# Five store tiles of 26, 25, 26, 25 and 26 tokens in place of 25, 25, 25, 25 and 28 in an expert-dispatch scaling kernel

## The chip, the core and the metric

The kernel runs on one core of one Trainium2 chip. The metric is the device time of one execution in microseconds. Three runs of the kernel before took 238.78, 238.79 and 238.80 us; their median is 238.79 us.

## What is computed

Each token's row of 512 floats is written out twice, once for each of its two experts, and multiplied by that expert's weight. The expert indices are not used.

```python
def reference(x, expert_indices, expert_weights):   # x (16, 1024, 512), expert_weights (16, 1024, 2), float32
    k = expert_indices.shape[-1]
    x_expanded = x[:, :, np.newaxis, :].repeat(k, axis=2)
    weights = expert_weights[..., np.newaxis]
    return (x_expanded * weights).astype(np.float32)   # (16, 1024, 2, 512)
```

There are 16,384 tokens, 128 for each of the chip's 128 partitions. The input is 33.6 MB and the output 67.1 MB, so the work is nearly all transfer.

## The kernel before

The 128 tokens of each partition are cut into five tiles, `groups` (L32). In this text a "token" of a tile means one token on every partition: 256 KiB to load and 512 KiB to store. The tiles are numbered from 0, and a tile's two stored halves are called a and b: store 0a, store 0b, and so on.

**Buffers.** `x_pair` holds two input buffers; tiles 0, 2 and 4 use the first (x0), tiles 1 and 3 the second (x1). There is a single output buffer, `o_ring`, `TX` = 25 tokens long (L33, L47). Every tile writes its products into the same `o_ring`, and its first 13 tokens (`CUT`, L34) are stored as one transfer, the rest up to `TX` as a second. So the products of the first half of one tile must wait until store a of the tile before has landed, and those of the second half until its store b has landed.

**Products.** For each half, VectorE takes the first 8 tokens (9 in tile 0) in instructions of up to four tokens (`vector`, L113; the instruction itself is L97), and ScalarE the remaining ones, two instructions for each token (`scalar`, L118, L120).

**Loads.** A tile's load is cut into the steps of `STEPS` (L35): tile 0 in 9 and 16 tokens, tile 2 in 21 and 4, tile 4 in 24 and 4. The two pieces are called load 0a, load 0b and so on here. Tiles 1 and 3 are loaded whole.

**Order.** All transfers but the first weights go through one queue, SyncE's, in program order (`move`, L65, which issues at L66): load 0a, load 0b, load 1, load 2a, load 2b, the weights of tiles 1 to 4, store 0a, store 0b, store 1a, store 1b, load 3, load 4a, load 4b, store 2a, store 2b, store 3a, store 3b, store 4a, store 4b. An issue that has to wait holds back all that follow it. Tiles 0 and 2 are "held" (L140): their two stores are issued only after the next load into the same input buffer, and each also waits until piece a of that load has landed (`wait`, L69, called at L156). Piece b of that load, 4 tokens, is then still in the queue.

**The third piece.** Tile 4 has 28 tokens, three more than `o_ring` holds. For these, VectorE makes one product of three tokens into the start of `o_ring` (L161), which waits until store 4a has landed, and a third store (L162), called store 4c here, ends the program.

Of the kernel before, what the change touches and what calls it, by code (L numbers as in the profile page):

```python
# [1 line left out]

# [4 lines left out]


@with_exitstack
def kernel(  # L10
    ctx: ExitStack,
    tc: tile.TileContext,
    x: bass.AP,
    expert_indices: bass.AP,
    expert_weights: bass.AP,
    out: bass.AP,
):
    nc = tc.nc

    batch, seq, hidden = x.shape  # L20
    k = expert_weights.shape[-1]
    P = nc.NUM_PARTITIONS
    ntok = batch * seq
    assert ntok % P == 0
    A_TOTAL = ntok // P

    f32 = mybir.dt.float32
    row = k * hidden
    CH = 4


    groups = [25, 25, 25, 25, 28]  # L32
    TX = 25  # L33
    CUT = 13  # L34
    STEPS = {0: [9, 16], 2: [21, 4], 4: [24, 4]}  # L35
    assert sum(groups) == A_TOTAL

    xf = x.rearrange("b s h -> (b s) h")
    of = out.rearrange("b s k h -> (b s) (k h)")
    wf = expert_weights.rearrange("b s k -> (b s) k")  # L40

    w_pool = ctx.enter_context(tc.tile_pool(name="w_pool", bufs=1))
    x_pool = ctx.enter_context(tc.tile_pool(name="x_pool", bufs=1))
    o_pool = ctx.enter_context(tc.tile_pool(name="o_pool", bufs=1))

    w_tile = w_pool.tile([P, A_TOTAL * k], f32)
    o_ring = o_pool.tile([P, TX * row], f32)  # L47
    x_pair = [
        x_pool.tile([P, max(groups[e::2]) * hidden], f32, name=f"x{e}")
        for e in range(2)  # L50
    ]

    def rows(of_all, done, T):
        return of_all[done * P : (done + T) * P, :].rearrange(
            "(p a) n -> p (a n)", a=T
        )

    tiles = []
    done = 0
    for n in groups:  # L60
        tiles.append((done, n))
        done += n


    def move(out, in_):  # L65
        return tc.keep_in_program_order(nc.sync.dma_start(out=out, in_=in_))  # L66


    def wait(ins, done):  # L69
        tc.add_manual_dep(  # L70
            ins.ins,
            done.ins.name,
            mybir.DependencyInfo(
                mybir.DependencyClass.Sync, mybir.DependencyReason.DATA
            ),
            reason="turn",
        )

    def load(i, e):
        at = sum(STEPS.get(i, groups[i : i + 1])[:e])  # L80
        to = at + STEPS.get(i, groups[i : i + 1])[e]
        part = slice(at * hidden, to * hidden)
        return move(x_pair[i % 2][:, part], rows(xf, *tiles[i])[:, part])

    def weights(g, to):
        at, n = tiles[g]
        w = w_tile[:, at * k : (at + (to - g) * n) * k]
        return (
            w.rearrange("p (g m) -> p g m", g=to - g),
            wf[at * P : (at + (to - g) * n) * P, :].rearrange(  # L90
                "(g p a) n -> p g (a n)", g=to - g, p=P
            ),
        )

    def product(o_tile, t, x_in, c, m):
        o = t * row
        nc.vector.tensor_tensor(  # L97
            out=o_tile[:, o : o + m * row].rearrange(
                "p (t k h) -> p t k h", t=m, k=k
            ),  # L100
            in0=x_in[:, : m * hidden]
            .rearrange("p (t h) -> p t h", t=m)
            .unsqueeze(2)
            .to_broadcast([P, m, k, hidden]),
            in1=w_tile[:, c : c + m * k]
            .rearrange("p (t k) -> p t k", t=m)
            .unsqueeze(3)
            .to_broadcast([P, m, k, hidden]),
            op=mybir.AluOpType.mult,
        )  # L110


    def vector(src, c, at, to):  # L113
        for t in range(at, to, CH):
            u = min(t + CH, to)
            product(o_ring, t, src[:, t * hidden : u * hidden], c + t * k, u - t)

    def scalar(src, c, at, to):  # L118
        return [
            nc.scalar.mul(  # L120
                out=o_ring[:, e * hidden : (e + 1) * hidden],
                in_=src[:, e // k * hidden : (e // k + 1) * hidden],
                mul=w_tile[:, c + e : c + e + 1],
            )
            for e in range(at * k, to * k)
        ]

    def store(dst, at, to):
        return move(dst[:, at * row : to * row], o_ring[:, at * row : to * row])


    out_w, in_w = weights(0, 1)
    nc.scalar.dma_start(out=out_w, in_=in_w)
    load(0, 0)
    load(0, 1)
    load(1, 0)
    for i, (done, n) in enumerate(tiles):
        src, dst, c = x_pair[i % 2], rows(of, done, n), done * k
        v = 9 if i == 0 else 8
        held = i in (0, 2)  # L140
        for at, to in [(0, CUT), (CUT, TX)]:
            vector(src, c, at, at + v)
            scalar(src, c, at + v, to)
            if not held:
                store(dst, at, to)
        if held:
            if i == 0:
                last = load(2, 0)
                load(2, 1)
                for g in range(1, len(tiles)):  # L150
                    move(*weights(g, g + 1))
            else:
                last = load(4, 0)
                load(4, 1)
            for at, to in [(0, CUT), (CUT, TX)]:
                wait(store(dst, at, to), last)  # L156
        elif i == 1:
            load(3, 0)
        if n > TX:
            m = n - TX  # L160
            product(o_ring, 0, src[:, TX * hidden :], c + TX * k, m)  # L161
            move(dst[:, TX * row :], o_ring[:, : m * row])  # L162

# [1 line left out]
_INS = ['x', 'expert_indices', 'expert_weights']  # L165
_OUTS = [((16, 1024, 2, 512), 'float32')]


# [23 lines left out]
```

## Time and profile before

| | |
|---|---|
| median of three runs | 238.79 us |
| the profiled execution: whole time | 238.92 us |
| the profiled execution: span, first to last instruction | 237.1 us |
| VectorE busy | 93.1 us (39%), 23 instructions |
| ScalarE busy | 54.9 us (23%), 87 instructions |
| SyncE's transfer queue (q1) | 3312 packets, 100.77 MB, 98.7% of 16 engines' span |
| mean rate over the span | 425 GB/s |

The time outside the span, 238.92 less 237.1, is 1.8 us. "98.7%" is the time that the packets of this queue took, summed, as a share of what 16 DMA engines have in the span. The rows that carry the argument are shown in the prediction.

### The profile page before, as it was taken

Reading aid. Unit: us, or ns where it says so; the run is one execution under the profiler, and the core shown is the slowest. Engines: PE = TensorE matmul, PEld = TensorE weight load, DVE = VectorE, ACT = ScalarE, POOL = GpSimd, SP = SyncE. Lnnn points to the kernel's source line nnn. Section 1 sums busy time; section 2 is a strip of 40 time slices with the busy share of each in tenths; the row PEclk is TensorE's granted clock in tenths of the full one; section 3 lists DMA queues with packets and bytes.
Section 4 is the critical chain, followed back from the end, with each engine's and each line's share of the span. In section 5 each row is a group of like instructions: output and inputs, shape, how many; then the busy total and the mean of one; then the engine's idle time right before and its main releaser. Section 6 shows DMA issues by size and latency. Waiting matters only on the chain.

```text
span 237.1 us, 217 instructions
## 1 busy us (share of the span) xinstructions
DVE 93.1 (39%) x23; ACT 54.9 (23%) x87; POOL 0.2 (0%) x4
## 2 busy tenths in 40 slices
DVE  0499800000094580954900000039195292861300
ACT  0008800000090520914400000037080270800000
POOL 0000000000000000000000000000000000000000
DMA  7999989899999999999999999999999999999996
GB/s 260 474 445 475 423 370 464 372 486 431 420 398 497 464 431 420 398 398 409 475 478 406 398 453 431 431 409 457 484 431 431 409 398 434 449 449 456 423 398 265
DMA packets 3457, 100.80 MB, mean 425 GB/s; under 512 B 1024, under 2 KB 1024, under 8 KB 1024
## 3 DMA queue, kind: packets, MB, share of 16 engines
q1 hardware_dynamic: 3312, 100.77, 98.7%
q10 hardware_dynamic: 144, 0.03, 0.1%
q14 instruction: 1, 0.01, 0.0%
HBM read 33.69 MB, written 67.11 MB: 425 GB/s over the span
## 4 chain that ended last, share of the span: by engine, by line
DMA 70%; DVE 16%; ACT 4%; issue 3%; SPq 0%; DVEq 0%; ACTq 0%
DMA out_dram<-o_ring 46%; DMA x<-in_x_dram 24%; DVE o_ring L97 16%; ACT o_ring L120 3%; ACT L120 1%; SPq L66 0%; DVEq L97 0%; ACTq L120 0%
## 5 line engine op out<-in xcount | busy, mean ns | idle before, releaser
L97 DVE TENSOR_TENSOR o_ring<-x,w_tile 128x4096 f32<-128x4096 f32 (+2 forms) x23 | 93.1, 4096 | 128.5 <-DMA out_dram<-o_ring 105.6
L120 ACT ACTIVATE o_ring<-x,w_tile 128x512 f32<-128x512 f32 x86 | 53.7, 709 | 134.0 <-DMA out_dram<-o_ring 123.3
L120 ACT ACT_TABLE_LOAD x1 | 1.3, 1283 | 18.6 <-DMA x<-in_x_dram 18.6
L176 POOL MEMSET const-bfloat16-1.0<- 128x1 bf16 x1 | 0.1, 102 | 0.0
L176 POOL MEMSET const-uint8-127<- 128x1 uint8 x1 | 0.1, 102 | 0.0
L176 POOL MEMSET const-float32-0.0<- 128x1 f32 x1 | 0.1, 99 | 0.2 <-issue 0.2
L176 POOL MEMSET const-float32-1.0<- 128x1 f32 x1 | 0.1, 99 | 0.0
## 6 DMA issues: line engine op xcount, KB each, us to landing
out_dram<-o_ring SPq DMA_DIRECT2D x5, 6656.0 KB, 21.3
out_dram<-o_ring SPq DMA_DIRECT2D x5, 6144.0 KB, 21.6
x<-in_x_dram SPq DMA_DIRECT2D x2, 6400.0 KB, 34.1
x<-in_x_dram SPq DMA_DIRECT2D x1, 6144.0 KB, 20.6
x<-in_x_dram SPq DMA_DIRECT2D x1, 5376.0 KB, 18.8
x<-in_x_dram SPq DMA_DIRECT2D x1, 4096.0 KB, 17.4
x<-in_x_dram SPq DMA_DIRECT2D x1, 2304.0 KB, 8.1
x<-in_x_dram SPq DMA_DIRECT2D x2, 1024.0 KB, 21.4
```

The source lines that it names most:

```text
L97: nc.vector.tensor_tensor(out=o_tile[:, o : o + m * row].rearrange("p (t k h) -> p t k h", t=m, k=k), in0=x_in[:, : m * hidden] .rearrange ...
L120: nc.scalar.mul(out=o_ring[:, e * hidden : (e + 1) * hidden], in_=src[:, e // k * hidden : (e // k + 1) * hidden], mul=w_tile[:, c + e : c ...
L176: nc = _bacc.Bacc("TRN2", target_bir_lowering=False, num_devices=1)
```

## The change

The tiles become 26, 25, 26, 25 and 26 tokens, and `o_ring` 26 tokens. Each tile now fits in it, so each is stored in two pieces: 13 and 13 tokens, or 13 and 12. The branch with the third piece goes. Piece b of load 0 has 17 tokens instead of 16, load 2 comes in 22 and 4 tokens instead of 21 and 4, and load 4 in 22 and 4 instead of 24 and 4. The number of tokens that VectorE takes is left as it is, so the added tokens of tiles 0, 2 and 4 fall to ScalarE, two instructions each. Input buffer x0 shrinks from 28 to 26 tokens.

```diff
-    groups = [25, 25, 25, 25, 28]
-    TX = 25
+    groups = [26, 25, 26, 25, 26]
+    TX = max(groups)
     CUT = 13
-    STEPS = {0: [9, 16], 2: [21, 4], 4: [24, 4]}
+    STEPS = {0: [9, 17], 2: [22, 4], 4: [22, 4]}
...
-        for at, to in [(0, CUT), (CUT, TX)]:
+        for at, to in [(0, CUT), (CUT, n)]:
             vector(src, c, at, at + v)
             scalar(src, c, at + v, to)
...
-            for at, to in [(0, CUT), (CUT, TX)]:
+            for at, to in [(0, CUT), (CUT, n)]:
                 wait(store(dst, at, to), last)
         elif i == 1:
             load(3, 0)
-        if n > TX:
-            m = n - TX
-            product(o_ring, 0, src[:, TX * hidden :], c + TX * k, m)
-            move(dst[:, TX * row :], o_ring[:, : m * row])
```

## The prediction

> **What bounds the kernel now.** I read the page's parts on the span and the queues first, because a kernel that moves 100 MB should be judged by how full its transfer queue is.
>
> ```profile
> span 237.1 us, 217 instructions
> ...
> DMA  7999989899999999999999999999999999999996
> ...
> q1 hardware_dynamic: 3312, 100.77, 98.7%
> ```
>
> The second line is the busy share of the 16 DMA engines in 40 slices of the span: nine tenths or more nearly throughout. 98.7% of 237.1 us is 234.0 us, so the engines stood idle for 3.1 us in all. The view by stretches says where. Its columns are start and end, length, the three compute engines with their counts, the granted TensorE clock, the DMA share and GB/s; packets count where they begin.
>
> ```profile
> 0.00:1.00 1.00, 0.00 (x0) 0.00 (x0) 0.20 (x4) 1.00 0.00 0
> 235.00:237.10 2.10, 0.00 (x0) 0.00 (x0) 0.00 (x0) 1.00 0.14 59
> ```
>
> The first microsecond moves nothing. In the last 2.1 us the share is 0.14, so 0.86 x 2.1 = 1.81 us are idle. Of the 3.1 us, 1.0 + 1.81 = 2.81 lie at the two ends, and about 0.3 us are left for everything between. So a change that keeps the bytes can gain about 0.3 us from gaps, and can lose as much as it opens.
>
> Now the chain that ended last, in order of time (start, length, what). It would mislead if it were read alone.
>
> ```profile
> 27.64 18.75 DMA x<-in_x_dram
> ...
> 46.41 18.56 DMA out_dram<-o_ring
> ...
> 118.85 20.61 DMA x<-in_x_dram
> ...
> 139.52 18.14 DMA out_dram<-o_ring
> ...
> 188.08 8.77 DVE o_ring L97 x2
> ...
> 196.90 21.27 DMA out_dram<-o_ring
> ...
> 218.29 3.36 DVE o_ring L97
> ```
>
> Its last link is the very product that the change removes, 3.36 us of VectorE after store 4a landed at 196.90 + 21.27 = 218.17. The chain follows releases, and a transfer in it counts from its issue, queueing included. Whether the product cost anything is decided by what the queue still held, so I take landing times: issue plus time to landing. The issues of the last three stores, and what each took to land (the middle one asked for at 211 to 212 us):
>
> ```profile
> 211.39 10.62 SPq L66 DMA_DIRECT2D out_dram<-o_ring  x2
> ...
> out_dram<-o_ring SPq DMA_DIRECT2D x1, 6144.0 KB, 21.3
> ...
> 221.68 0.33 SPq L66 DMA_DIRECT2D out_dram<-o_ring  x1
> ...
> out_dram<-o_ring SPq DMA_DIRECT2D x1, 1536.0 KB, 14.7
> ```
>
> Store 4b landed at 211.39 + 21.3 = 232.69, store 4c at 221.68 + 14.7 = 236.38. Store 4c was thus issued 11.0 us before the queue was through with 4b. The product and the wait in front of it are covered.
>
> **The price of a byte.** From 218.17 to 232.69 the queue carried the 6144 KiB of store 4b and nothing else: 14.52 us, 433 GB/s. One token costs 0.605 us to load and 1.21 us to store. Thirteen stored tokens cost 15.73 us, four loaded ones 2.42.
>
> **What goes away.** The last store took 236.38 - 232.69 = 3.69 us for three tokens, which at the price above are 3.63. Its own packets, 3312 / 23 = 144 for one of the queue's 23 transfers, cost 0.06 us more. The same from the queue's view of the stretch 231.7 to 235.2, small packets, and then 142 to 156, large ones:
>
> ```profile
> DMA packets 135, 1.50 MB, mean 428 GB/s; under 512 B 13, under 2 KB 13, under 8 KB 13
> ...
> q1 hardware_dynamic: 135, 1.50, 100.4%
> ...
> DMA packets 112, 5.96 MB, mean 426 GB/s; under 512 B 0, under 2 KB 0, under 8 KB 0
> ...
> q1 hardware_dynamic: 112, 5.96, 98.3%
> ```
>
> 428 / 1.004 = 426.3 GB/s and 426 / 0.983 = 433.4 GB/s: 1.6% of 3.69 us is again 0.06. With the rounding of the landing times it is 0 to 0.12; I take **-0.06 us**. The product (3.36 us) and its issue go at no gain, because the cover is 11.0 us.
>
> The Trainium skill, SBUF — State Buffer, section "The DMA setup-cost knee", says that every transfer pays a roughly fixed 2 us, and advises the largest single transfers. By it one transfer less would give -2.0 us where it stands in line. The rows above leave 0.06: behind another transfer the fixed part is not seen.
>
> **What moves.** The bytes stay. Loads: tile 0 gains a token, tile 2 one (25 to 26 in all), tile 4 loses two. Stores: 0b, 2b and 4b grow by one token each, 3 x 1.21 = 3.63 us, the bytes of 4c. So the queue runs 0.61 us late after load 0b, 1.21 after load 2a, 2.42 after store 0b, 1.21 again after load 4a, 2.42 after store 2b, 3.63 after store 4b, where it ends and 4c used to follow: sum **0**, as long as no new gap opens. What each issue waits for, and what is in the queue meanwhile:
>
> ```profile
> 9.01 19.70 DVE L97 TENSOR_TENSOR o_ring<-x,w_tile 128x4096 f32<-128x4096 f32 x6 [9.01 <-DMA w_tile<-in_expert_weights_dram]
> ...
> 19.90 8.68 ACT L120 ACTIVATE o_ring<-x,w_tile 128x512 f32<-128x512 f32 x14
> ...
> 27.64 1.48 SPq L66 DMA_DIRECT2D x<-in_x_dram  x2
> 29.16 1.90 SPq L66 DMA_DIRECT2D w_tile<-in_expert_weights_dram  x4
> ...
> 1.16 0.90 SPq L66 DMA_DIRECT2D x<-in_x_dram  x2
> ...
> x<-in_x_dram SPq DMA_DIRECT2D x1, 6400.0 KB, 32.0
> ```
>
> *Tile 0.* Load 1 was issued by 2.06 and landed 32.0 us later, at 33.6 or after; it begins 0.61 later now. Load 2a, of 22 tokens, must also wait for VectorE's one-token product, whose end bounds the six: 9.01 + 19.70 = 28.71, at most 0.61 later, 29.3, against 27.64. That is 4.9 us before load 1 lands (34.2), more than the way from an issue to its bytes takes (2.65 us at most, below): hidden. ScalarE has 16 instructions for 14, 8.68 / 14 = 0.62 us each: it ends at 19.90 + 0.61 + 9.92 = 30.4, when load 2b can go; behind it on SyncE stand the four weight transfers (1.9 us of issuing) and store 0a, none of which is wanted before load 2a lands at 46.39 + 1.21 = 47.6. Hidden.
>
> *The two held stores.* Store 0a waits for load 2a, store 2a for load 4a, and only the four tokens of piece b, 2.42 us, keep the queue busy. Landing to landing (start plus length in the chain): 46.39 to 64.97 is 18.58 = 15.73 + 2.42 + 0.43, the last for the four weight transfers; 139.46 to 157.66 is 18.20 = 15.73 + 2.42 + 0.05. So no gap now, to 0.05 us. Piece b keeps four tokens at both places; load 4a gets shorter, which moves the wait and not its cover. Cost 0. If the cover failed, what would be needed is 0.06 from landing to issue, plus the way from issue to landing beside the bytes. The latter is bounded by the first load and row one above: over 0.27 us (issued at 0.73, nothing by 1.00), and at most 8.1 - 9 x 0.605 = 2.65:
>
> ```profile
> 0.73 0.38 SPq L66
> ...
> x<-in_x_dram SPq DMA_DIRECT2D x1, 2304.0 KB, 8.1
> ```
>
> The gap is then 2.65 + 0.06 - 2.42 = 0.29 us at worst at each place, 0.58 for both; the sums above put it at 0, and I take that.
>
> *The halves.* A half is computed after the store in its part of `o_ring` has landed (8.77 us in the chain, 0.05 to the issue at 196.90, and 0.12 from the landing at 218.17 to the start at 218.29) while the other half's store, 14.52 or 15.73 us, is running. The margin is at least 14.52 - 8.94 = 5.6 us, 2.9 after the 2.65 for the way; the change only lengthens covers (0b, 2b). ScalarE's added pair makes ten instructions in a second half:
>
> ```profile
> 172.38 5.01 ACT L120 ACTIVATE o_ring<-x,w_tile 128x512 f32<-128x512 f32 x8 [8.01 <-DMA out_dram<-o_ring]
> ...
> 188.07 6.24 ACT L120 ACTIVATE o_ring<-x,w_tile 128x512 f32<-128x512 f32 x10 [10.68 <-issue]
> ```
>
> 6.24 us, still under VectorE's 8.77. The scheduler puts the added pair of tiles 2 and 4 early, right behind tiles 1 and 3 on ScalarE, where it waits for piece b of its load. Queued behind it are the next tile's first products, which wait for a landing until 188.07 anyway, and the pair of tile 4 comes behind 172.38 + 5.01 = 177.4, while load 4b is ahead of store 2a in the queue, which landed at 157.66. Cost 0.
>
> **The sum.** -0.06 us on the profiled execution, 238.92 to 238.86; on the median, 0.13 lower, **238.73 us**. What a measurement can tell from no change is about 0.2%, 0.48 us: the forecast is no measurable change.
>
> **The rivals.**
>
> *A gap behind the held stores (slower).* If the landings of the 16 engines drift further apart, or an issue takes longer, the four tokens no longer cover the way, and store 0a and store 2a begin late. For: it is the thinnest cover of the kernel, and the change does not thicken it. Against: the two sums with 0.05 us left. At the bound, 0.58 us: 239.3. It passes 0.2% when the two gaps together exceed 0.54 us, and does so only at the very end of the bound. 0.07, of which I count 0.06 as slower.
>
> *A slower stride (slower).* Tiles of 26 give each partition a pitch of 104 KiB in the output and 52 KiB in the input, which the kernel has not had (100 and 50, 112 and 56). 78 of 128 tokens would be affected, 0.61 x 234.0 = 143 us; 1% there gives 1.4 us, 240.2, and 0.34% decides. Against: VectorE starts a half right when a store lands, so the stores' landings stand in its starts:
>
> ```profile
> 172.39 8.76 DVE L97 TENSOR_TENSOR o_ring<-x,w_tile 128x4096 f32<-128x4096 f32 x2 [5.77 <-DMA out_dram<-o_ring]
> ...
> 188.08 8.76 DVE L97 TENSOR_TENSOR o_ring<-x,w_tile 128x4096 f32<-128x4096 f32 x2 [6.93 <-issue]
> ...
> 202.57 8.76 DVE L97 TENSOR_TENSOR o_ring<-x,w_tile 128x4096 f32<-128x4096 f32 x2 [5.73 <-DMA out_dram<-o_ring]
> ```
>
> Store 3a, pitch 100, took 188.08 - 172.39 = 15.69 us; store 4a, pitch 112, 218.29 - 202.57 = 15.72. Both have 13 tokens, and the pitches on both sides of 104 give one rate. 0.04.
>
> *The last link was real (faster).* If the product, 3.36 us, and the issue behind it, 0.33, were on the path as the chain draws it, the time would be 238.79 - 3.7 = 235.1. For: the chain. Against: 11.0 us of cover, and 2.8 of the 3.1 idle us lie in the first and the last two, where the first transfer must still begin and the last one still land. 0.02.
>
> *A transfer has a fixed part that the queue doesn't hide (faster).* Its bound is the way found above, 2.65 us: 238.79 - 2.65 = 236.1. For: the first load shows it, with nothing in front of it. Against: the 0.06 us of store 4c behind 4b, and the 0.05 that store 2a and load 4b leave. 0.02. The rule of the Trainium skill, SBUF — State Buffer, "The DMA setup-cost knee", would give 236.8 by its 2 us; the trace doesn't agree where transfers queue.
>
> *The change does not do what it says.* The third piece is gone from the program, so this one falls in with the forecast: it shortens a link that ends nothing.
>
> **How the numbers follow.** Forecast 0.85, gap 0.07, stride 0.04, last link 0.02, fixed part 0.02. Faster are the last two, 0.04; slower the gap's 0.06 and the stride's 0.04, together 0.10; within 0.2% 0.86. The likeliest time is 238.73. The range: low, 0.12 for the packets and the 0.3 us of idle time in the middle, 238.79 - 0.12 - 0.3 = 238.4; high, one gap at its bound, 238.73 + 0.29 = 239.0. It leaves out the two faster and slower ends, under 0.2 together.
>
> **What would show it.** Right: the queue's share stays at 98.7% or a tenth more, with 144 packets fewer (3168); landing to landing, store 0a is 18.6 and store 2a 18.2 us behind its load; store 4b, now 13 tokens, lands some 15.7 us behind 4a and ends the transfers near 236.3; load 2a is issued at 28.7 to 29.3 and lands near 47.6; store 2a lands near 157.66 + 1.21 = 158.9. Wrong: one of the two sums over 18.9, which is a gap; 13 tokens of a 26-token tile taking more than 15.8 us, which is the stride; or a span below 236.5, which would mean that the third piece stood on the path.

## The result, and the profile after

The changed kernel took 239.55 us (median of 10 runs, 239.22 to 240.44) beside 238.78 us for the kernel before (10 runs, 238.74 to 238.81): ratio 1.0038, 95% interval 1.0026 to 1.0049. It is slower, and its runs differ by 1.2 us where those of the kernel before differ by 0.07. Measured twice more, in the experiments below, the medians were 239.35 and 239.33 beside 238.99 and 238.97: ratios 1.0019 (1.0011 to 1.0028) and 1.0013 (1.0004 to 1.0022).

The profiled execution took 239.49 us. Its page, the span, the busy share of the DMA engines and the queue:

```profile
span 237.7 us, 218 instructions
...
DMA  7999998999999999999999999999999999999996
...
q1 hardware_dynamic: 3168, 100.77, 98.7%
```

By these lines nothing has happened: 144 packets fewer, the same bytes, the same 98.7%. The loss shows in the landing times. A transfer's landing is the moment when the last of its bytes has arrived. The chain that ended last, in order of time (start, length, what):

```profile
1.15 18.46 DMA x<-in_x_dram
...
29.60 18.49 DMA x<-in_x_dram
...
48.10 18.56 DMA out_dram<-o_ring
...
91.29 21.23 DMA out_dram<-o_ring
...
121.43 19.97 DMA x<-in_x_dram
...
141.47 18.10 DMA out_dram<-o_ring
```

The first link of the kernel before, which the prediction did not show, is this one:

```profile
1.16 17.37 DMA x<-in_x_dram
```

*First place, the start.* Load 0b landed at 1.15 + 18.46 = 19.61 us, before at 18.53. Its one added token accounts for 0.61; 0.47 us are lost. Load 2a, due near 47.6 by the forecast, landed at 48.09, still 0.49 late.

*Second place, the switch from storing to loading.* The queue changes over once, from store 1b to load 3. The first product of tile 2 starts right when store 1a lands, so from there to the landing of load 4a the queue carries store 1b, load 3 and load 4a. These are the timeline's rows of that product, before and then after:

```profile
95.24 8.76 DVE L97 TENSOR_TENSOR o_ring<-x,w_tile 128x4096 f32<-128x4096 f32 x2 [6.93 <-issue]
```

```profile
98.12 8.76 DVE L97 TENSOR_TENSOR o_ring<-x,w_tile 128x4096 f32<-128x4096 f32 x2 [6.90 <-issue]
```

Before: 139.46 - 95.24 = 44.22 us, against 14.52 + 15.13 + 14.52 = 44.17 by bytes: 0.05 lost. After: 141.40 - 98.12 = 43.28, against 14.52 + 15.13 + 13.31 = 42.96: 0.32 lost. Below, these two figures are called the start loss (load 0b against 18.53, or 19.14 with 17 tokens) and the switch loss. Counted from the landing of store 1a itself, the switch loss is 0.08 larger in both kernels, as one of the expectations below has it for the kernel before (0.13).

*The rest runs as forecast.* Store 0a landed 48.10 + 18.56 - 48.09 = 18.57 us behind load 2a, store 2a 159.57 - 141.40 = 18.17 us behind load 4a: no gap at the held stores. The end, the issue of stores 4a and 4b, and what 4a and then 4b took to land:

```profile
199.86 14.84 SPq L66 DMA_DIRECT2D out_dram<-o_ring  x2
```

```profile
out_dram<-o_ring SPq DMA_DIRECT2D x1, 6656.0 KB, 21.3
...
out_dram<-o_ring SPq DMA_DIRECT2D x1, 6656.0 KB, 22.5
```

Store 4a landed at 221.16; 4b, issued at 199.86 + 14.84 - 0.33 = 214.37, at 236.87, 15.7 us later, as its bytes ask. Start 0.47, switch 0.32 - 0.05 and the packets -0.06 make 0.68 us; measured are 239.49 - 238.92 = 0.57. The other 0.11 was regained at store 2b, by a loss of the kernel before that the changed one did not have. From the landing of store 2a to the first product that waits for store 2b, the kernel before took 172.39 - 157.66 = 14.73 us for 14.52 us of bytes, the changed one 175.34 - 159.57 = 15.77 for 15.73; that is 0.17, and 0.06 went again on the way to the end.

```profile
175.34 8.76 DVE L97 TENSOR_TENSOR o_ring<-x,w_tile 128x4096 f32<-128x4096 f32 x2 [6.82 <-DMA out_dram<-o_ring]
```

The trace's own packet and landing records say what the two places have in common. The 128 large packets of a transfer, one for each partition, are split over 16 engines, eight on each, and the transfer lands when the last engine is through. Load 0a landed 0.54 us apart on the first and the last engine before, 1.01 us after. At the switch, the engines' last packets of store 1b (1.815 us each as a rule) took longer: summed over the 16 engines, 1.8 us before and 8.6 after. A stretched packet counts as busy, which is why the share of 98.7% hides it.

This sum is not the loss; most of it falls on engines that are ahead. The engine that had been last was not held up at store 1b at all. But two others, 0.52 and 0.89 us ahead of it, took 0.96 and 1.28 us longer for their last packet of store 1b and their first of load 3 (1.891 us as a rule), more than their lead, and with load 3 these two landed last. The switch costs time only where an engine pays more than its lead.

### The profile page after: what moved, and what is told of

Same layout as the page of the kernel before. It is cut to its first block, busy times and chain, and to the rows that moved or that the text cites. A ratio compares the mean times of both kernels' runs of the same rounds, so it can differ in the third digit from the quotient of the medians.

```text
span 237.7 us, 218 instructions
## 1 busy us (share of the span) xinstructions
DVE 89.9 (38%) x22; ACT 58.6 (25%) x93; POOL 0.2 (0%) x4
## 3 DMA queue, kind: packets, MB, share of 16 engines
q1 hardware_dynamic: 3168, 100.77, 98.7%
## 4 chain that ended last, share of the span: by engine, by line
DMA 70%; DVE 13%; ACT 4%; DVEq 2%; issue 0%; SPq 0%; ACTq 0%
DMA out_dram<-o_ring 46%; DMA x<-in_x_dram 24%; DVE o_ring L97 13%; ACT o_ring L120 4%; DVEq L183 2%; ACT L120 1%; SPq L66 0%; DVEq L97 0%; ACTq L120 0%
## 5 line engine op out<-in xcount | busy, mean ns | idle before, releaser
L97 DVE TENSOR_TENSOR o_ring<-x,w_tile 128x4096 f32<-128x4096 f32 (+1 forms) x22 | 89.9, 4131 | 124.4 <-DMA out_dram<-o_ring 100.8
L120 ACT ACTIVATE o_ring<-x,w_tile 128x512 f32<-128x512 f32 x92 | 57.3, 709 | 132.2 <-DMA out_dram<-o_ring 122.8
```

Of the source, the lines that this page charges most:

```text
L97: nc.vector.tensor_tensor(out=o_tile[:, o : o + m * row].rearrange("p (t k h) -> p t k h", t=m, k=k), in0=x_in[:, : m * hidden] .rearrange ...
L120: nc.scalar.mul(out=o_ring[:, e * hidden : (e + 1) * hidden], in_=src[:, e // k * hidden : (e // k + 1) * hidden], mul=w_tile[:, c + e : c ...
```

## The experiments

The theories at the start: **S**, the first reads of tile 0 are uneven since its rows lie 52 KiB apart; **W**, the first weights, in rows of 208 bytes, disturb load 0a; **O**, the loss comes at the stores or the switch. Unless said otherwise the differences are to the changed kernel, and medians stand with their lowest and highest run. The groups of runs below were taken on different chips; each is compared with runs of the kernel before on the same chip.

**The changed kernel again, the row distance, the weights.** The kernel before took 238.99 us here (33 runs, 238.78 to 239.19 and one of 239.76).

> The changed kernel once more. In its first profile load 0b lands 0.47 us later than its one added token explains (19.61 us, where 18.53 + 0.61 = 19.14 was due), and the last store ends about that much too late. Theory S (the first reads, of tile 0, run unevenly with rows 52 KiB apart): time 239.2 to 240.4 again, with a spread of tenths, and the profiled execution's excess over 238.73 us stands already in the landing of load 0b. Theory O (the stores with rows 104 KiB apart, or the change from storing to loading before load 3): the same time, but load 0b near 19.14 in any execution that is slow.

239.35 us (239.02 to 239.95). The profiled execution, 239.22 us, has a start loss of 0.15 and a switch loss of 0.30: both places at once, so neither S nor O by itself.

```diff
# load0_pitch25
+        if i == 0:
+            from_ = slice(0, 9 * hidden) if e == 0 else slice(8 * hidden, 25 * hidden)
+            return move(x_pair[0][:, part], rows(xf, 0, 25)[:, from_])
```

> The changed kernel, only tile 0's two load pieces read rows 50 KiB apart instead of 52 (same bytes, same sizes; tile 0 then works on other tokens than it should). Theory S: 238.7 us, spread under 0.1, load 0b landing near 19.1. Theory W (the first weights, rows of 208 bytes instead of 200): unchanged, 239.2 to 240.4. Theory O: unchanged.

239.13 us (238.95 to 239.91), ratio to the kernel before 1.0013 (1.0004 to 1.0021). The start loss is gone from the chain, 1.16 + 18.02 - 19.14 = 0.04:

```profile
1.16 18.02 DMA x<-in_x_dram
```

But three of eleven runs were still at 239.58 or more, so S is not the whole. The median is 0.22 us lower, with runs that overlap; that S is a part of the time is not shown by it.

```diff
# before_load0_pitch26, to the kernel before
+        if i == 0:
+            return move(x_pair[0][:, part], rows(xf, 0, 26)[:, part])
```

> The kernel before, only tile 0's two load pieces read rows 52 KiB apart instead of 50 (tile 0 then works on other tokens than it should). Theory S: 239.3 to 240.3 us with a spread of tenths, load 0b landing later than 18.53. Theories W and O: 238.8, spread under 0.1.

239.04 us (238.87 to 239.36), ratio 1.0004 (0.9994 to 1.0013): no difference in the time, against S's 239.3. The start loss is there, 1.16 + 17.67 - 18.53 = 0.30:

```profile
1.16 17.67 DMA x<-in_x_dram
```

```diff
# before_w52, to the kernel before
-    out_w, in_w = weights(0, 1)
+    out_w = w_tile[:, : 26 * k]
+    in_w = wf[: 26 * P, :].rearrange("(p a) n -> p (a n)", p=P)
```

> The kernel before, only the first weights are read as rows of 52 floats instead of 50 (tile 0 then multiplies by other weights). Theory W: 239.3 to 240.3 us, with a spread of tenths. Theories S and O: 238.8, spread under 0.1.

238.99 us (238.78 to 239.06), ratio 0.9999 (0.9990 to 1.0008). W falls.

**The addresses of all loads.** Each load got a table entry with its start, row distance and first token; the kernel before took 238.97 us (34 runs, 238.81 to 239.16).

```diff
-        return move(x_pair[i % 2][:, part], rows(xf, *tiles[i])[:, part])
+        base, pitch, first = READ[i][e]
+        from_ = slice(first * hidden, (first + to - at) * hidden)
+        return move(x_pair[i % 2][:, part], rows(xf, base, pitch)[:, from_])
```

> The changed kernel beside the three that follow, on the same chip. It gives the size of the loss there. In the two profiles so far the last engine's landing is late at two places: at load 0a (0.2 to 0.5 us) and between store 1b and load 3 (0.37 us, where the kernel before loses 0.13). Theory H (both are costs of reads that begin together, and depend on the addresses they begin at) and theory N (the second is not a matter of addresses): some 0.3 to 0.8 us over the kernel before.

239.33 us (239.04 to 239.79). The profiled execution was the slowest, 239.79: start loss 0.31, switch loss 0.75.

> The changed kernel, every load at the start addresses and row distances of the kernel before (sizes and order as changed; the tiles then work on other tokens than they should). Theory H: within 0.1 us of the kernel before, no tail of slow runs. Theory N: 0.15 us or more over the kernel before, and the landing of load 3 still loses 0.3 us or more against store 1b's.

239.18 us (238.97 to 239.96), ratio 1.0014 (1.0004 to 1.0023), five of twelve runs at 239.40 or more. The profiled execution took 239.77 us:

```profile
97.82 8.76 DVE L100 TENSOR_TENSOR o_ring<-x,w_tile 128x4096 f32<-128x4096 f32 x2 [6.90 <-issue]
```

```profile
121.45 20.13 DMA x<-in_x_dram
```

121.45 + 20.13 - 97.82 = 43.76 against 42.96: a switch loss of 0.80 with every load at its old start address and row distance, while load 0b (19.29) lost 0.15. Theory H, that the loads' addresses make the switch slow, falls.

> The changed kernel, only load 3 at the start address it has in the kernel before (2 tokens of every partition earlier; its row distance is the same 50 KiB in both; tile 3 then works on other tokens than it should). Theory H with the base address as its cause: about 0.15 to 0.25 us less than the changed kernel, and load 3 loses about 0.13 us against store 1b. Theory N: as the changed kernel.

239.33 us (239.07 to 239.93): as the changed kernel, load 3's address is not it.

> The kernel before, every load at the start addresses and row distances of the changed one (sizes, stores and third piece as before; the tiles then work on other tokens than they should). Theory H: 0.3 to 0.8 us over the kernel before, like the changed kernel. Theory N: 0.05 to 0.3 us over it, from load 0a alone.

239.13 us (238.86 to 239.25), ratio 1.0005 (0.9996 to 1.0013), start loss 0.13, switch loss 0.26. H falls from this side too: no run is over 239.25, and 0.16 us over the kernel before is what N expected from load 0a alone.

**Halves of the change.** The kernel before took 239.00 us (15 runs, 238.84 to 239.23).

```diff
-    groups = [26, 25, 26, 25, 26]
-    STEPS = {0: [9, 17], 2: [22, 4], 4: [22, 4]}
+    groups = [25, 25, 25, 25, 26]                   # last26
+    STEPS = {0: [9, 16], 2: [21, 4], 4: [22, 4]}
+    groups = [26, 25, 25, 25, 26]                   # first26
+    STEPS = {0: [9, 17], 2: [21, 4], 4: [22, 4]}
+    groups = [25, 25, 26, 25, 26]                   # third26
+    STEPS = {0: [9, 16], 2: [22, 4], 4: [22, 4]}
```

> Tiles of 25, 25, 25, 25 and 26 tokens, buffers as in the changed kernel, no third piece; the last two tokens of every partition are left out (126 of 128). By bytes and packets 2 x 1.815 + 0.06 = 3.69 us under the kernel before: 235.28 where that is 238.97. Theory B (the losses come with the places where the buffers lie on the chip, or with the missing third piece): 0.3 us more, 235.6, and runs up to 236.3. Theories T0 and T2 (they come with a tile 0, or a tile 2, of 26 tokens): 235.3, spread as the kernel before, under 0.4.

235.32 us (4 runs, 235.30 to 235.44). The forecast's sum, bytes and 0.06 us for the packets of the third piece, gives 235.31 from the 239.00 beside it. The 0.06 by itself is too small to tell from nothing here.

> Tiles of 26, 25, 25, 25 and 26 tokens, the last token of every partition left out (127 of 128). By bytes and packets 1.815 + 0.06 = 1.88 us under the kernel before: 237.09 where that is 238.97. Theory T0 (tile 0 of 26 tokens: its first reads, and all that follow lie one token further): 237.4, runs up to 238.1. Theory T2: only load 0a's 0.1 to 0.2 us, 237.25, no run over 237.5. Theory B: 237.4 and a tail.

237.61 us (5 runs, 237.27 to 238.09): 0.5 over the bytes. The profiled execution was the slowest, with a start loss of 0.32 and a switch loss of 0.76.

> Tiles of 25, 25, 26, 25 and 26 tokens, the last token of every partition left out (127 of 128); tiles 0 and 1 lie where they do in the kernel before. 237.09 by bytes and packets. Theory T0: 237.1, spread as the kernel before. Theory T2 (the change from storing to loading before load 3 gets worse by what ScalarE or the tile after it does): 237.3 and runs up to 238. Theory B: 237.4 and a tail.

237.15 us (5 runs, three of 237.15, then 237.73 and 238.00): the sum by bytes, and two runs far above it.

```diff
# before_store1_moved, to the kernel before
-        src, dst, c = x_pair[i % 2], rows(of, done, n), done * k
+        src, dst, c = x_pair[i % 2], rows(of, 26 if i == 1 else done, n), done * k
```

> The kernel before, only the stores of tile 1 go to the addresses they have in the changed kernel (a token per partition further; one region is written twice and one not at all). Theory T0 in the form that store 1b's addresses make the handover to load 3 slow: 0.15 to 0.3 us over the kernel before, runs up to 239.9. Otherwise: as the kernel before.

239.04 us (238.88 to 239.32), ratio 1.0001 (0.9992 to 1.0010): store 1b's address is not it.

**The halves again, with as many bytes as the kernel before.** It took 238.98 us (29 runs, 238.75 to 239.24).

```diff
+    more = 6 * hidden                               # last26_filled; 3 * hidden in the other two
+    move(rows(of, 0, groups[0])[:, :more], o_ring[:, :more])
```

> Tiles of 25, 25, 25, 25 and 26 tokens in the changed kernel's buffers, the last two tokens of every partition left out, and three tokens stored once more at the end (over the first tokens of tile 0), so that the queue carries as many bytes as in the kernel before: 239.0 us by bytes and packets. Theory B (where the buffers lie): a tail, 3 or 4 runs of 11 over 239.4. Theories T0 and T2: none over 239.3.

239.01 us (238.89 to 239.21), ratio 1.0002 (0.9994 to 1.0011): theory B falls, buffers and third piece are cleared. Its profiled execution has a switch loss of 0.49 all the same (118.86 + 19.83 - 95.24 = 43.45 against 42.96) and took 239.12 us:

```profile
95.24 8.76 DVE L96 TENSOR_TENSOR o_ring<-x,w_tile 128x4096 f32<-128x4096 f32 x2 [6.91 <-issue]
```

```profile
118.86 19.83 DMA x<-in_x_dram
```

> Tiles of 26, 25, 25, 25 and 26 tokens, one token of every partition left out, one and a half stored once more at the end: 239.0 us by bytes and packets. Theory T0 (tile 0): median 239.3 to 239.5, runs up to 240. Theory T2 alone: median 239.1 to 239.2, none over 239.4. Theory B: a tail.

239.20 us (238.94 to 240.28), ratio 1.0019 (1.0007 to 1.0030), five of twelve runs at 239.53 or more.

> Tiles of 25, 25, 26, 25 and 26 tokens, one token of every partition left out, one and a half stored once more at the end: 239.0 us by bytes and packets. Theory T2 (something of tile 2 that stands ahead of load 3): median 239.0, 3 or 4 runs of 11 over 239.4, late at the landing of load 3. Theory T0: none over 239.3. Theory B: a tail.

239.17 us (238.94 to 240.43), ratio 1.0019 (1.0005 to 1.0033), four of twelve runs at 239.62 or more. Tile 0 and tile 2 each bring the long runs by themselves; T0 and T2 as alternatives both fall.

**Where the long runs lose, and whether row distance is needed.** The kernel before took 238.95 us (19 runs, 238.84 to 239.17).

> Tiles of 25, 25, 26, 25 and 26 tokens, filled up, once more, for its tail and a second profile: 3 or 4 runs of 12 over 239.4. Theory M (a late engine falls further behind when the queue changes from store 1b to load 3): if the profiled execution is one of the slow ones, its last engine loses 0.5 us or more there, between the landings of store 1b and load 3. Theory P (rows 52 or 104 KiB apart slow the transfers of tile 2 themselves): the loss stands at load 2a or at stores 2a and 2b.

239.09 us (238.89 to 240.14), four of twelve runs at 239.56 or more. The profiled execution was one of them, 239.83 us:

```profile
95.92 8.76 DVE L96 TENSOR_TENSOR o_ring<-x,w_tile 128x4096 f32<-128x4096 f32 x2 [6.91 <-issue]
```

```profile
119.89 20.16 DMA x<-in_x_dram
```

119.89 + 20.16 - 95.92 = 44.13 against 42.96: a switch loss of 1.17 us, more than the whole excess over 238.95. Its page shows as little of it as that of the changed kernel:

```profile
span 238.1 us, 217 instructions
...
DMA  7999989899999999999999979999999999999996
...
q1 hardware_dynamic: 3312, 100.77, 98.5%
```

One slice, that of 136.9 to 142.9 us, is at seven tenths, and the share is 0.2 points lower. In the packet records this is a gap behind load 4b: store 2a, issued at 140.10 when load 4a had landed, came too late for 14 of the engines, which then stood idle for 0.3 to 0.6 us. The engines that were last did not wait, so the gap added nothing to the time. Up to store 1a this execution had kept within 0.1 us of the kernel before. M holds in its place, not in its mechanism: in the packet records two engines took 1.02 and 0.93 us longer for their last packet of store 1b and neither had been the last one. Theory P, slow rows of tile 2, falls.

```diff
# before_load2a_22, to the kernel before
-    STEPS = {0: [9, 16], 2: [21, 4], 4: [24, 4]}
+    STEPS = {0: [9, 16], 2: [22, 4], 4: [24, 4]}
...
+        if (i, e) == (2, 1):
+            return move(x_pair[0][:, part], rows(xf, *tiles[i])[:, 21 * hidden : 25 * hidden])
```

> The kernel before, load 2a one token longer (22 instead of 21, row distance as before; piece b starts a token later in the buffer, so tile 2 works partly on other tokens). 0.61 us more by bytes: 239.6. Theory X (the loss comes from what the added token ahead of load 3 does to the queue: sizes and times, no row distance): 3 or 4 runs of 11 over 240.0. Theory P: none over 239.9.

239.61 us (7 runs: six from 239.56 to 239.67 and one of 240.09).

```diff
# before_load0b_17, to the kernel before
+        if (i, e) == (0, 1):
+            to += 1
+            part = slice(at * hidden, to * hidden)
+            from_ = slice((at - 1) * hidden, (to - 1) * hidden)
+            return move(x_pair[0][:, part], rows(xf, *tiles[i])[:, from_])
```

> The kernel before, load 0b one token longer (17 instead of 16, row distance as before; the piece is read one token earlier, so tile 0 works partly on other tokens). 0.61 us more by bytes: 239.6. Theory X: 3 or 4 runs of 11 over 240.0. Theory P: none over 239.9.

239.70 us (5 runs: 239.53, 239.55, 239.70, 239.81, 240.51). Together two of twelve runs lie over 240.0, where X wanted three or four of eleven each and P none over 239.9. The kernel before, in all its 130 runs beside these experiments, was over its median by 0.4 us or more only once, by 0.77. So one more token ahead of load 3 can bring a long run without any new row distance; with so few of them this leans to X and does not settle it.

**All profiles together.** For the 20 profiled executions of all these kernels I set the spread of load 0a's landings over the 16 engines against the time by which the last packets of store 1b were stretched, summed over the engines. Their rank correlation (1 would be the same order in both) is 0.89: spreads of 0.44 to 0.56 us go with 1.2 to 2.0 us, spreads of 0.63 to 1.01 with 2.1 to 8.6. In the spread, eight executions that read tile 0 with rows 52 KiB apart had 0.72 to 1.01 us, the twelve with 50 KiB 0.44 to 0.84. This is an order found in the profiles: engines that set out unevenly are stretched more at the switch. That the one causes the other was not tried by itself.

The time that is lost there follows less closely. Between the spread and the switch loss the rank correlation is 0.51: load3_as_before had a stretch of 4.1 us and a switch loss of 0.00, third26_again 3.5 and 1.17. What the profiles do bear out is that nothing much is lost elsewhere: in all 20, start loss and switch loss, less the 0.05 of the kernel before, together come within 0.3 us of the whole excess, that is, of the time over what bytes and packets give from 238.92 us.

## Why the prediction was wrong

**"The sum: -0.06 us", "no measurable change".** Wrong. 239.55 us lies outside 238.4 to 239.0, on the slower side, to which I gave 0.10.

**"What goes away", -0.06 us.** It fits. last26 came out at 235.32 where the bytes and these 0.06 give 235.31, and last26_filled, which ends with a transfer of three tokens again, equals the kernel before; the 0.06 alone lies within the runs' spread. The product and its wait were covered, as argued; the rivals of the last link and of the fixed part fall. The Trainium skill's 2 us for each transfer (SBUF — State Buffer, section "The DMA setup-cost knee") is not seen here either, for a transfer behind another.

**"What moves", sum 0 "as long as no new gap opens".** This step failed. It priced a transfer by its bytes at 433 GB/s and looked for idle time, and no idle time came: the share is still 98.7%. What grew is the time of single packets on single engines. It was mis-sized at two places: load 0b, priced at 0.61 us for its token, came 0.47 later still in the profiled execution (0.15 and 0.31 in the two others of the changed kernel); and the switch from store 1b to load 3, priced at nothing beside its bytes, lost 0.32, and 0.75 to 1.17 in the long executions that were profiled. The Trainium skill, Perfetto Trace Analysis, section "What "DMA-bound" means", names specific DMA engines as the first thing that can bind such a kernel. The traces agree: load 0a landed 1.01 us apart on the engines at an unchanged mean share.

**About 0.3 us of idle time in the middle.** A misreading, which the sum does not use but the low end of the range does. The view by stretches counts a packet where it begins, so its share of 0.14 leaves out what began before 235.0. By the packet records of the kernel before, an engine began at 1.91 us on average and was through 1.24 us before the end; these two are already all of the idle time, and nothing is left for the middle.

**"A gap behind the held stores."** Not there: 18.57 and 18.17 us, as in the kernel before. (In third26_again it opened on the engines that were ahead, where it costs nothing.) Its premise, that the engines drift further apart, came true; but the price was paid at a place I had not looked at, where no issue is late.

**"A slower stride."** Wrong as stated: 13 tokens of a 26-token tile took 15.7 us, and neither the loads' addresses nor store 1b's, each changed by itself, brought the long runs. Where row distance does show is in the very first reads, on which I had no row of 26 tokens: the landing spread of load 0a. By itself, in before_load0_pitch26, it moves the median by 0.05 us, within the interval.

**"The halves", tile 0's waits and ScalarE's pair.** Right: load 2a was issued at 29.60, the forecast's 28.7 to 29.3 and the start loss on top, over 5 us before load 1 landed, and the queue never ran dry for want of a product.

What stays open is why a 26-token tile 0 or tile 2 makes the bad switches frequent. Cleared, each by itself, are the first weights, the loads' addresses, store 1b's address, the buffers' places and the third piece. What is left is what else a token more ahead of load 3 changes in sizes and moments.

## What to carry to other kernels

Where a queue is full, judge a change by the landing times of the transfers against their bytes, place by place, and not by the busy share: the share is a mean over 16 engines, and a stretched packet counts as busy. Look first at the points where many engines turn at once. Here these were the first reads and the change from storing to loading; the two changes from loading to storing (18.57 and 18.17 us) lost nothing. Each transfer here was cut into equal shares, so what the last engine lost was not made up by the others. And compare the spread of the runs, not only their median: in the half-changed kernels one execution in three carried nearly all of the loss.

## What the runs showed of the hardware

- A change from storing to loading in a full queue stretched the last stored packets, of 1.815 us each, by 1.2 to 8.6 us summed over the 16 engines, and a single one by up to 1.06 us (third26_filled). The time lost by it was 0.00 to 1.17 us. The Trainium skill, DMA: Bandwidth & Descriptors, section "Latency and other measured facts", gives an access to the main memory 0.2 us on average and 2 us at high load; the longest single stretch lies between these, and no run here shows that it is this latency.
- The first reads of a launch landed 0.44 to 1.01 us apart on the 16 engines, and much the same unevenness was still there when store 1a landed (1.01 and then 0.99 us in the changed kernel).
